# The seam before the last MLP by halves of the tokens, and where the last down weights are split

## The chip, the core and the metric

The kernel runs on one core of a Trainium2 chip. The time is device microseconds of one execution of the whole program; a lower one is better. A profiled execution gives the trace from which all rows below are taken. Five kinds of work appear in it: TensorE (PE, with its weight loads PEld apart), VectorE (DVE), ScalarE (ACT), GpSimd (POOL, hardly used here) and SyncE (SP), whose queue issues nearly all loads.

## What is computed

The reference is a two-layer backbone over 256 latent tokens and 256 context tokens, 1024 wide. Layer 0 mixes by a Conformer convolution, layer 1 by a bidirectional mLSTM with four heads. Each mixer and each MLP closes with a norm:

```python
h = layer_norm(ALPHA * h + g1 * y, ln1_g[i], ln1_b[i])
h = layer_norm(ALPHA * h + g2 * sq_relu_mlp(modulate(h, sh2, sc2), mlp_w1[i], mlp_w2[i]), ln2_g[i], ln2_b[i])

def sq_relu_mlp(u, w1, w2):
    return jnp.square(jax.nn.relu(u @ w1)) @ w2
```

The change lies at the end of layer 1, where only the 256 latent tokens are left: the mixer's last product (`y @ w_down`, one quarter of its input rows for each head), the norm over it, and the MLP (1024 to 4096 to 1024) with the last norm.

## The kernel before

Every f32 operand is split in two fp32r parts, a high one (ScalarE's cast, L154) and a low one (VectorE's subtraction, L155), and a product is taken as high x high, high x low and low x high. Weights come in raw tiles of 1 MB (`raw_load`, L148; three buffers, tag `raw`), each holding two pieces of 128x1024; `split_w` (L160) splits a piece into a `wh` and a `wl` tile (four buffers each, `NW`), or, if it is given a maker, into four tiles of 128x512 from that maker's pool. Nothing in the program fixes the order on an engine, but for a few marked places: a planner lays the instructions of each engine in a list ahead of time, by program order as priority and by its own estimates of when an operand is ready; the chip then runs each list in order. A tile made in a pool waits for the release of the tile that had its place.

The mixer's end is `down(h)` (L1371), once for each head: four k tiles, each with products for two token halves t (128 tokens) and two column halves h_ (512 columns), all into four PSUM banks `dacc`. Heads 0 to 2 run interleaved with the attention of head 3 (`Z.att`, last entry). Then four pieces of the MLP's first weights are loaded and split (`pre1`, L1431), and only then does `down(3)` load and split its weights, into the `XL` pool, whose sixteen tiles held the input of the output gate (`gate_o`, L1293) until the last gate was done. `down(3)` runs one (t, h_) after the other, and after each VectorE scales, adds and takes statistics (L1398 to L1400). `root` (L1410) makes mean and reciprocal deviation, L1445 normalizes in place, and L1448 transposes the tokens into four banks `trs` (two `ln`, two `cv`), each of which holds two of the eight feature tiles for both token halves. When both halves are in, `affine_half` (L492) makes each of the eight MLP inputs `u2[f]`: two ScalarE passes from PSUM over 256 tokens (L496) and a VectorE subtraction (L497); a `u2` tile holds the high part in columns 0 to 255 and the low part behind it.

The MLP's first four hidden tiles are made together: k tile outermost, four PSUM banks (three `mm`, one `fl`, the same that `dacc` had). `up_mm` (L1468) takes w high x both parts of u2 in one product of 512 columns (L1470) and w low x u2 high in one of 256 (L1471). `up_out` (L1479) adds the two halves, squares the positive part and splits it into `hid`. The loop then goes in steps of two hidden tiles m: `up(m)`, `up(m+1)`, `dn(m-4)`, `dn(m-3)`, where `dn` (L1513) adds a hidden tile's product with w2 to four banks `facc`. At m = 6 VectorE scales the residual by the rows `ln1g` and `ln1b` (L1537, L1538); these rows are loaded after the mixer's pool is closed. The last four `dn` run by (t, h_), each followed by the epilogue L1545 to L1547; after each token half come `root`, L1551, L1552 and the store.

Of the kernel before, what the change touches and what calls it, by code (L numbers as in the profile page):

```python
# [15 lines left out]
P = 128  # L16
# [7 lines left out]
H = 4  # L24
# [48 lines left out]
def hybrid_kernel(ctx: ExitStack, tc: tile.TileContext, xT, vecs_d, cc_d, rows_d, wdw_d, ada0_w, ada_w, ada1_w, wg_d, pw1a, pw1, pw2, w1_0, w2_0,  # L73
# [74 lines left out]
    def raw_load(src):  # L148
        raw = wp.tile([P, 2048], F32, tag="raw", name=nm("raw"), bufs=3)
        nc.sync.dma_start(raw[:, :src.shape[-1]], src)  # L150
        return raw
# [1219 lines left out]
    def down(h):  # L1371
        if h == 0:
            for t in range(2):
                for h_ in range(2):
                    dacc[t, h_] = psum("fl" if t and h_ else "mm")
            for h_ in range(2):
                g1r.append(PW())
                nc.sync.dma_start(g1r[h_], row(g_dr[0][h_ * T:(h_ + 1) * T]))
        last = h == H - 1
        ws = []  # L1380
        for q in range(2):
            raw = raw_load(wdown[h, q])
            for i in range(2):
                w = split_w(raw[:, i * D:(i + 1) * D], XL if last else None)
                ws.append(w if last else tuple([v_[:, h_ * T:(h_ + 1) * T] for h_ in range(2)] for v_ in w))
                if not last:
                    kt = 2 * q + i
                    for t in range(2):
                        for h_ in range(2):
                            down_mm(h, kt, t, h_, ws[kt])  # L1390
                    yield
        if last:
            for t in range(2):
                for h_ in range(2):
                    for kt in range(4):
                        down_mm(h, kt, t, h_, ws[kt])
# [4 lines left out]
                    yield  # L1401

    def down_mm(h, kt, t, h_, w):
        yh, yl = yy[h][kt]
# [31 lines left out]
    trs = []  # L1436
    last = down(H - 1)
    for t in range(2):
        for h_ in range(2):
            next(last)  # L1440
        root(mv1[:, t], st1[:, t])
        if t == 0:
            trs = [psum(n_) for n_ in ("ln", "ln", "cv", "cv")]
        for h_ in range(2):
            nc.vector.tensor_scalar(hl[t][h_], hl[t][h_], mv1[:, t, 0:1], mv1[:, t, 2:3], op0=ALU.subtract, op1=ALU.mult)  # L1445
            for j in range(4):
                f = 4 * h_ + j
                nc.tensor.transpose(trs[f // 2][:, f % 2 * C + t * P:f % 2 * C + (t + 1) * P],  # L1448
                                    hl[t][h_][:, j * P:(j + 1) * P], ident)
    for _ in last:  # L1450
        pass
    close_pool()

    ca, cb = comb(1, "ln1_g1", "ln1_b1", "sc2", "sh2", (1,))
    qf = open_pool("qf")
    U, HD = maker(qf, "u", DT), maker(qf, "hid", 8)
    u2 = []
    for f in range(DT):
        t = U(F32R)
        affine_half(t[:, LO], t[:, HI], trs[f // 2][:, f % 2 * C:f % 2 * C + C], 1, ca, cb, f)  # L1460
        u2.append(t)
# [32 lines left out]
    def weights2(j):  # L1494
        if j % 2 == 0:
            raws["d"] = raw_load(w2_1[j // 2])
        return split_w(raws["d"][:, j % 2 * D:(j % 2 + 1) * D])

    def up(m):
        w, ps = weights1(m), psum()  # L1500
# [15 lines left out]
            for h_ in range(2):  # L1516
                fin_mm(j, t, h_, w)

    pss = [psum("fl" if m == 3 else "mm") for m in range(4)]
    for kt in range(DT):  # L1520
        for m in range(4):
            up_mm(pss[m], pre1[m], kt)
    for m in range(4):
        up_out(m, pss[m])
    for t in range(2):
        for h_ in range(2):
            facc[t, h_] = psum("cv" if t else "ln")
    for m in range(4, NF, 2):
        up(m)
        up(m + 1)  # L1530
        dn(m - 4)
        dn(m - 3)
        if m == 6:
            for t in range(2):
                for h_ in range(2):
                    r, sl = hl[t][h_], slice(h_ * T, (h_ + 1) * T)
                    nc.vector.scalar_tensor_tensor(r, r, ALPHA, ln1g[:, sl], op0=ALU.mult, op1=ALU.mult)  # L1537
                    nc.vector.scalar_tensor_tensor(r, ln1b[:, sl], ALPHA, r, op0=ALU.mult, op1=ALU.add)  # L1538
    ws = [weights2(j) for j in range(NF - 4, NF)]
    for t in range(2):  # L1540
        for h_ in range(2):
            for j in range(NF - 4, NF):
                fin_mm(j, t, h_, ws[j - NF + 4])
            tm, r, sl = tmp("E"), hl[t][h_], slice(h_ * T, (h_ + 1) * T)
            nc.vector.tensor_tensor(tm, facc[t, h_], g2r[:, sl], op=ALU.mult)  # L1545
            nc.vector.tensor_tensor(r, r, tm, op=ALU.add)
            nc.vector.bn_stats(st1[:, t, h_, :], r)  # L1547
# [86 lines left out]
```

## Time and profile before

| | |
|---|---|
| median of three runs | 1727.58 us (1720.66, 1727.64, 1727.58) |
| the profiled execution | 1725.27 us, its span 1723.6 us |
| mean granted TensorE clock | 0.991 |
| PE busy | 1681.7 us (98%), 9450 products |
| DVE busy | 1052.4 us (61%) |
| ACT busy | 730.0 us (42%) |
| DMA | 301.64 MB, 175 GB/s in the mean |

A row of the timeline gives start and length in us, the engine, the line of the kernel, the operation with output and inputs, the shape, and in brackets how long the engine stood idle before it and what released it. A product's length covers its passage through the array, so lengths overlap, and the pace is read from the starts. A row of the windows gives busy time and number of instructions for each engine, then the granted TensorE clock, the share of time that the DMA engines were busy, and GB/s. A row of groups gives busy time, mean ns of one, and the idle time before.

### The profile page before, as it was taken

The numbers are of one execution on the slowest core, as the hardware profiler recorded it, in microseconds if no ns is written. First come the engines' busy times: TensorE is split into PE (matmuls) and PEld (weight loads), VectorE is DVE, ScalarE is ACT, GpSimd is POOL, SyncE is SP. The second block draws the span as 40 slices with busy tenths as digits, with TensorE's granted clock in tenths as the row PEclk, the third lists the DMA queues.
The fourth block names the chain that finished last, engine by engine and source line by source line (L and its number), as shares of the span: only waits on it lengthen the run. The fifth ranks groups of instructions, "written<-read, shape, count | busy, mean of one in ns | idle before, by whom it ended". The sixth has DMA issues, their size and how long they took to land.

```text
span 1723.6 us, 23808 instructions
## 1 busy us (share of the span) xinstructions
PE 1681.7 (98%) x9450; PEld 1400.1 (81%) x9450; DVE 1052.4 (61%) x1887; ACT 730.0 (42%) x1148; POOL 33.6 (2%) x84
## 2 busy tenths in 40 slices
PE   8999999999999999999999999999999999979997
PEld 5655798888888999986688999998777878868886
DVE  5456897975665776772132443443487776677666
ACT  3311763231324465542232432442476574445542
POOL 0000000000000000000000000000010110000000
PEclk9999999999999999999999999999999999989999
DMA  9323533665556055568653642343345555456552
GB/s 362 139 109 123 216 127 146 221 220 158 207 220 169 28 165 171 170 214 281 235 193 101 216 146 98 121 149 147 138 171 204 183 210 205 171 183 220 189 185 90
DMA packets 62687, 301.64 MB, mean 175 GB/s; under 512 B 8115, under 2 KB 22963, under 8 KB 29169
## 3 DMA queue, kind: packets, MB, share of 16 engines
q1 hardware_dynamic: 42832, 285.44, 47.0%
q10 hardware_dynamic: 19744, 14.69, 2.6%
q8 instruction: 74, 1.21, 0.3%
q14 instruction: 37, 0.30, 0.0%
HBM read 284.37 MB, written 15.74 MB: 174 GB/s over the span
## 4 chain that ended last, share of the span: by engine, by line
PE 91%; DVE 4%; ACT 2%; DMA 1%; issue 1%; POOL 0%; SPq 0%; DVEq 0%; ACTq 0%; POOLq 0%
PE mm L177 19%; PE mm L181 19%; PE mm L180 19%; PE mm L1470 3%; PE mm L185 3%; PE mm L187 3%; PE mm L186 3%; PE mm L1471 2%; PE cv L185 1%; PE cv L187 1%; PE cv L186 1%; PE fl L297 1%; DVE wl L155 1%; PE fl L647 1%; PE cv L716 1%; PE ln L177 1%
## 5 line engine op out<-in xcount | busy, mean ns | idle before, releaser
L155 DVE TENSOR_TENSOR wl<-raw,wh 128x1024 fp32r<-128x1024 f32 x350 | 427.0, 1223 | 357.0 <-ACT wh L154 354.4
L154 ACT CAST wh<-raw 128x1024 fp32r<-128x1024 f32 x350 | 364.9, 1050 | 560.6 <-PE mm L180 347.8
L180 PE MATMUL mm<-u,wh 128*128 128x256 f32 (+1 forms) x1152 | 376.9, 327 | 0.0
L177 PE MATMUL mm<-u,wh 128*128 128x256 f32 (+1 forms) x1024 | 328.2, 321 | 5.8 <-DVE E L673 2.9
L181 PE MATMUL mm<-u,wl 128*128 128x256 f32 (+1 forms) x1024 | 327.0, 320 | 0.0
L180 PEld LDWEIGHTS mm<-u,wh 128*128 128x128 f32 x1152 | 220.6, 192 | 18.1 <-DVE mv L482 0.8
L177 PEld LDWEIGHTS mm<-u,wh 128*128 128x128 f32 x1024 | 196.2, 192 | 27.6 <-issue 8.9
L181 PEld LDWEIGHTS mm<-u,wl 128*128 128x128 f32 x1024 | 196.4, 192 | 15.9 <-DVE wl L155 1.7
L177 PE MATMUL mm<-xm,wh 128*128 128x512 f32 x256 | 102.8, 402 | 0.0
L185 PE MATMUL mm<-wh,xl 128*128 128x512 f32 x256 | 101.3, 397 | 0.7 <-ACT wh L154 0.5
L186 PE MATMUL mm<-wh,xl 128*128 128x512 f32 x256 | 100.5, 392 | 0.6 <-DVE xl L155 0.6
L181 PE MATMUL mm<-xm,wl 128*128 128x512 f32 x256 | 100.3, 392 | 0.0
L187 PE MATMUL mm<-wl,xl 128*128 128x512 f32 x256 | 99.6, 394 | 0.3 <-DVE wl L155 0.2
L177 PE MATMUL mm<-hid,wh 128*128 128x512 f32 (+1 forms) x256 | 94.0, 367 | 2.2 <-ACT hid L154 2.2
L180 PE MATMUL mm<-hid,wh 128*128 128x512 f32 (+1 forms) x256 | 93.8, 367 | 0.1
L181 PE MATMUL mm<-hid,wl 128*128 128x512 f32 (+1 forms) x256 | 93.6, 366 | 0.0
L1470 PE MATMUL mm<-u,wh 128*128 128x512 f32 x248 | 89.2, 402 | 1.4 <-DVE u L497 1.0
L357 DVE CUSTOM_DVE_ANT_0 raw<-raw,cb,vecs 128x1024 f32<-128x1024 f32 x48 | 61.1, 1281 | 33.9 <-DMA raw<-ada_w 33.6
L180 PE MATMUL mm<-qq,wh 128*128 128x272 f32 x256 | 73.9, 289 | 0.0
L177 PE MATMUL mm<-qq,wh 128*128 128x272 f32 x256 | 73.9, 289 | 0.0
L181 PE MATMUL mm<-qq,wl 128*128 128x272 f32 x256 | 73.8, 288 | 0.0
L177 PEld LDWEIGHTS mm<-xm,wh 128*128 128x128 f32 x256 | 48.1, 188 | 22.5 <-issue 6.7
(462 smaller groups left out, 3064.2 us busy)
## 6 DMA issues: line engine op xcount, KB each, us to landing
raw<-w SPq DMA_DIRECT2D x64, 1024.0 KB, 4.8
raw<-ada_w SPq DMA_DIRECT2D x48, 1024.0 KB, 5.0
raw<-wo SPq DMA_DIRECT2D x32, 1024.0 KB, 4.8
raw<-wv SPq DMA_DIRECT2D x16, 1024.0 KB, 5.4
raw<-wqT SPq DMA_DIRECT2D x16, 1024.0 KB, 5.6
raw<-wq SPq DMA_DIRECT2D x16, 1024.0 KB, 4.8
raw<-wk SPq DMA_DIRECT2D x16, 1024.0 KB, 4.9
raw<-pw SPq DMA_DIRECT2D x10, 1024.0 KB, 7.0
```

The source lines that it names most:

```text
L154: c = nc.scalar.copy(hi, src)
L155: nc.vector.tensor_tensor(lo, src, hi.bitcast(F32), op=ALU.subtract)
L177: a = nc.tensor.matmul(ps, wh, xh, start=start, stop=False)
L180: nc.tensor.matmul(ps, wh, xl, start=False, stop=False)
L181: nc.tensor.matmul(ps, wl, xh, start=False, stop=stop)
L185: nc.tensor.matmul(ps, xh, wh, start=start, stop=False)
L186: nc.tensor.matmul(ps, xl, wh, start=False, stop=False)
L187: nc.tensor.matmul(ps, xh, wl, start=False, stop=stop)
L297: a = nc.tensor.matmul(ps[32 * j:32 * j + 32], cs[:, kt, 14 - 2 * v:46 - 2 * v], blocks[kt], start=first and kt < 4, stop=last and kt >= 4 ...
L357: nc.vector.tensor_tensor_reduce(dump, w, cb[:, s, :], 1.0, vecs[:, o:o + 1], ALU.mult, ALU.add, accum_out=ada[1][:, m, s:s + 1])
L1470: a = lambda stop: nc.tensor.matmul(ps, wh, u2[kt], start=kt == 0, stop=stop)
L1471: b = lambda: nc.tensor.matmul(ps[:, LO], wl, u2[kt][:, LO], start=False, stop=False)
```

## The change

1. `down(1)` loads the raw tiles of `down(3)`'s weights beside its own and splits them into the `XL` tiles, piece by piece behind its own products; `down(3)` then only multiplies.
2. `u2` lies in the pool of `x` tiles, which outlives the mixer's pools, and is made by token halves (`u2_half`), with 128 columns an operation. `turn(0)` and `u2_half(0)` stand ahead of the second token half's `down(3)` products in the program. The first four hidden tiles are made by `first(t, ...)`: for one token half, a product of 256 columns (128 tokens, high and low) and one of 128. The transposes `turn(1)` are issued behind the products of k tile 5 of the first half.
3. For the second token half the fourth hidden tile's products come after those of the other three.
4. The scaling of the residual moves from m = 6 to m = 8 and is tied there: its first instruction keeps its place in the program, and the others are issued behind it.
5. The pieces of w2 for j = 24 to 27 are loaded and split at m = 16 and 18 into sixteen tiles of their own (`wx`). `dn` is left out for j = 24 to 27; the last eight j run at the end: first token half with both column halves, then the second token half by column halves, each with its epilogue behind it.
6. `hid` has ten buffers instead of eight.

```diff
@@ down(h)
+        if h == H - 1:
             for t in range(2):
                 for h_ in range(2):
                     for kt in range(4):
-                        down_mm(h, kt, t, h_, ws[kt])
+                        down_mm(h, kt, t, h_, wlast[kt])
...
+        for q in range(2):
+            raw = raw_load(wdown[h, q])
+            if h == 1:
+                rawl = raw_load(wdown[H - 1, q])
+            for i in range(2):
...
+                        down_mm(h, 2 * q + i, t, h_, w)
+                if h == 1:
+                    wlast.append(split_w(rawl[:, i * D:(i + 1) * D], XL))
+                yield
@@ the seam
+    ca, cb = comb(1, "ln1_g1", "ln1_b1", "sc2", "sh2", (1,))
+    u2 = [X(F32R) for _ in range(DT)]
+
+    def u2_half(t):
+        for f in range(DT):
+            src = trs[f // 2][:, f % 2 * C + t * P:f % 2 * C + (t + 1) * P]
+            hi, lo, y = u2[f][:, t * P:(t + 1) * P], u2[f][:, C + t * P:C + (t + 1) * P], tmp("S")[:, :P]
+            for o_ in (hi, y):
+                nc.scalar.activation(o_, src, AF.Identity, scale=ca[:, 1, f:f + 1], bias=cb[:, 1, f:f + 1])
+            nc.vector.tensor_tensor(lo, y, hi.bitcast(F32), op=ALU.subtract)
+
+    def up_half(ps, w, kt, t):
+        wh, wl = kcol(w, kt)
+        v = lambda z_: z_.rearrange("p (s t) -> p s t", s=2)[:, :, t * P:(t + 1) * P]
+        a = lambda stop: nc.tensor.matmul(v(ps), wh, v(u2[kt]), start=kt == 0, stop=stop)
+        b = lambda: nc.tensor.matmul(ps[:, t * P:(t + 1) * P], wl, u2[kt][:, t * P:(t + 1) * P], start=False, stop=False)
+        if kt < DT - 1:
+            a(False)
+            return b()
+        b()
+        return a(True)
+
+    def first(t, grp, kts):
+        for kt in kts:
+            for m in grp:
+                a = up_half(pss[m], pre1[m], kt, t)
+        return a
+
+    def turn(t):
+        for h_ in range(2):
+            for j in range(4):
+                f = 4 * h_ + j
+                nc.tensor.transpose(trs[f // 2][:, f % 2 * C + t * P:f % 2 * C + (t + 1) * P],
+                                    hl[t][h_][:, j * P:(j + 1) * P], ident)
...
+        for h_ in range(2):
+            nc.vector.tensor_scalar(hl[t][h_], hl[t][h_], mv1[:, t, 0:1], mv1[:, t, 2:3], op0=ALU.subtract, op1=ALU.mult)
         if t == 0:
             trs = [psum(n_) for n_ in ("ln", "ln", "cv", "cv")]
+            turn(0)
+            u2_half(0)
     for _ in last:
         pass
+    pss += [psum("fl" if m == 3 else "mm") for m in range(4)]
+    mid = first(0, range(4), range(6))
+    with tc.issue_after(mid.ins):
+        turn(1)
+    first(0, range(4), range(6, DT))
+    u2_half(1)
+    first(1, range(3), range(DT))
+    first(1, (3,), range(DT))
     close_pool()
@@ the loop and the tail
     for m in range(4, NF, 2):
         up(m)
         up(m + 1)
-        dn(m - 4)
-        dn(m - 3)
+        if m < NF - 4:
+            dn(m - 4)
+            dn(m - 3)
+        if m == 8:
+            ops = scaled()
+            first = tc.keep_in_program_order(next(ops))
+            with tc.issue_after(first.ins):
+                for _ in ops:
+                    pass
+        if 16 <= m < 20:
+            for j in (NF - 24 + m, NF - 23 + m):
+                wend[j] = weights2(j, WX)
+    for j in range(NF - 4, NF):
+        w = weights2(j)
+        wend[j] = tuple([v_[:, h_ * T:(h_ + 1) * T] for h_ in range(2)] for v_ in w)
     for t in range(2):
+        for hs_ in ([(0, 1)] if t == 0 else [(0,), (1,)]):
+            for j in range(NF - 8, NF):
+                for h_ in hs_:
+                    yh = hid[j]
+                    mm3t(facc[t, h_], yh[:, t * P:(t + 1) * P], yh[:, C + t * P:C + (t + 1) * P], wend[j][0][h_], wend[j][1][h_],
+                         False, j == NF - 1)
```

`scaled` issues the same eight instructions as L1537 and L1538 before; `weights2(j, WX)` passes the maker to `split_w`.

More of the change, by code (lines that the diff above doesn't have):

```diff
@@ L1517, in dn @@
                 fin_mm(j, t, h_, w)
[L1519 to L1522, printed above, removed]
     for m in range(4):
@@ L1527, in hybrid_kernel, with scaled @@
             facc[t, h_] = psum("cv" if t else "ln")
+    def scaled():
+        for t in range(2):
+            for h_ in range(2):
+                r, sl = hl[t][h_], slice(h_ * T, (h_ + 1) * T)
+                yield nc.vector.scalar_tensor_tensor(r, r, ALPHA, ln1g[:, sl], op0=ALU.mult, op1=ALU.mult)
+                yield nc.vector.scalar_tensor_tensor(r, ln1b[:, sl], ALPHA, r, op0=ALU.mult, op1=ALU.add)
+    wend = {}
     for m in range(4, NF, 2):
```

49 lines of the change are left out of this document (10 added, 39 removed).

## The prediction, made before the changed kernel was run

> **What bounds the kernel now.** I read the windows first: for most of the span TensorE has no gap, and what can be won lies where it has one.
>
> ```profile
> core 0: us, PE busy (x) PEld busy (x) DVE busy (x) ACT busy (x) POOL busy (x), PEclk, DMA share, GB/s
> 1508.80:1512.80 4.00, 0.23 (x2) 0.02 (x1) 2.98 (x4) 2.10 (x4) 0.00 (x0) 1.00 0.88 373
> 1512.80:1526.80 14.00, 13.98 (x56) 10.46 (x56) 12.15 (x21) 3.97 (x8) 0.00 (x0) 0.88 0.69 259
> 1603.00:1614.08 11.08, 11.08 (x58) 9.41 (x57) 7.27 (x10) 5.55 (x8) 0.00 (x0) 1.00 0.55 192
> ```
>
> The row at 1603 is one step of the MLP loop (two `up`, two `dn`): TensorE full, VectorE 7.27 of 11.08 us. The rows above it are the seam, where TensorE stands still and then runs at a granted clock of 0.88. Next the timeline of TensorE through the seam:
>
> ```profile
> 1508.62 0.39 PE L187 MATMUL fl<-wl,x 128*128 128x512 f32 x1
> 1512.78 0.78 PE L185 MATMUL mm<-xl,og 128*128 128x512 f32 x1 [3.77 <-ACT xl L154]
> 1513.36 0.63 PE L186 MATMUL mm<-xl,og 128*128 128x512 f32 x1
> ...
> 1519.90 0.39 PE L187 MATMUL mm<-xl,og 128*128 128x512 f32 x1
> ...
> 1525.07 0.63 PE L1448 MATMUL ln<-ident,hl 128*128 128x128 f32 x4
> 1525.54 0.60 PE L1448 MATMUL cv<-ident,hl 128*128 128x128 f32 x4
> ...
> 1526.43 0.40 PE L187 MATMUL fl<-xl,og 128*128 128x512 f32 x1
> 1530.42 1.12 PE L1448 MATMUL ln<-ident,hl 128*128 128x128 f32 x4 [3.59 <-DVE hl L1445]
> 1533.41 0.79 PE L1470 MATMUL mm<-u,wh 128*128 128x512 f32 x1 [1.02 <-DVE u L497]
> ...
> 1537.80 0.39 PE L1470 MATMUL mm<-u,wh 128*128 128x512 f32 x1
> 1538.03 0.28 PE L1471 MATMUL mm<-u,wl 128*128 128x256 f32 x1
> 1538.15 0.39 PE L1470 MATMUL mm<-u,wh 128*128 128x512 f32 x1
> ...
> 1545.90 0.39 PE L1470 MATMUL fl<-u,wh 128*128 128x512 f32 x1
> 1546.66 0.50 PE L1470 MATMUL mm<-u,wh 128*128 128x512 f32 x1 [0.37 <-ACT wh L154]
> 1547.92 0.39 PE L1471 MATMUL mm<-u,wl 128*128 128x256 f32 x1 [0.76 <-DVE wl L155]
> ```
>
> Starts are closer than durations, since products overlap: 0.23 us for 512 columns (1537.80 to 1538.03), 0.12 for 256 (1538.03 to 1538.15), so 0.35 for a pair L1470 and L1471. After the 3.77 us gap a product of 512 columns lasts 0.63 us where it lasts 0.39 later, so 0.24 is lost with each: half speed. From 1508.85 (the last product of the third `down` done) to 1546.13 (the last first product) 37.3 us pass, for 48 x 0.227 + 16 x 0.105 + 32 x 0.35 = 23.8 us of work. The 13.5 us between are three waits and the slow clock after them.
>
> **The change, part by part.** I lay the new order on the time axis of this trace. The sum is made against the profiled execution, 1725.27 us (span 1723.6 and 1.67 around it); the median of the runs shown, 1727.58, is 2.3 above it, and those runs spread over 7 us (1720.66 to 1727.64).
>
> *Last w_down split early.* The first wait follows from the load order:
>
> ```profile
> L155 DVE TENSOR_TENSOR wl<-raw,wh 128x1024 fp32r<-128x1024 f32 x350 | 427.0, 1223 | 357.0 <-ACT wh L154 354.4
> L154 ACT CAST wh<-raw 128x1024 fp32r<-128x1024 f32 x350 | 364.9, 1050 | 560.6 <-PE mm L180 347.8
> ...
> 1491.83 0.33 SPq L150 DMA_DIRECT2D raw<-wdown  x1
> 1507.24 0.89 SPq L150 DMA_DIRECT2D raw<-wdown  x2
> raw<-wdown SPq DMA_DIRECT2D x8, 1024.0 KB, 4.8
> ACT wh L154 <- PE fl L186: 16.7, 6, 4.4
> ```
>
> With two loads of 4.8 us moved ahead of the third `down` and of `pre1` on SP's queue, the 3.77 us and the half speed behind it go. What is late next is the last head's own output, whose low half VectorE ends at 1510.6 (the next fence); two of four k tiles are ready by then, which last 6 x 0.227 = 1.4 us, to 1510.2. I put 0.5 us there. The 8 casts and 8 subtractions of 512 columns (at most 0.7 each, as L155 in the next fence) move into a stage where ScalarE waits 16.7 us in six waits for TensorE: nothing. But three raw buffers now carry two more loads before those of the third `down`. Its first load takes the buffer of a moved one; that one lands about 1484.5 and needs four casts and subtractions, so I estimate 1489.5, landing at 1494.3, split (1.05 and 1.22, the two rows on top) by 1496.7. The first use, counted back from 1508.85 by 48 x 0.227 and eight transposes, is 1497.1. If it gets the buffer freed at 1491.83 instead, it is 1.9 us late, and twice that if the other is late too. Bounds 0 and 3.8 us lost; I take 0.7, as the near case just fits.
>
> *Half norms.*
>
> ```profile
> 1509.92 0.68 DVE L155 TENSOR_TENSOR og<-og,og 128x512 fp32r<-128x512 f32 x1
> 1531.72 1.29 DVE L1537 SCALAR_TENSOR_TENSOR hl<-hl,row 128x512 f32<-128x512 f32 x2 [0.90 <-DMA row<-rows_d]
> 1531.69 0.56 ACT L496 ACTIVATE S<-ln,cb,ca 128x256 f32<-128x256 f32 x1
> 1532.14 0.56 ACT L496 ACTIVATE u<-ln,cb,ca 128x256 fp32r<-128x256 f32 x1
> 1497.62 1.52 ACT L1347 ACTIVATE og<-og,gmv 128x512 f32<-128x512 f32 x2
> L1257 DVE TENSOR_TENSOR S<-S,x 128x128 f32<-128x128 f32 x8 | 2.3, 281 | 0.0
> ```
>
> Tokens 0 to 127 end at 1508.85 + 0.5 + 24 x 0.227 = 1514.8. Today their norm takes 5.0 us (1520.1 to the transposes at 1525.07), so `turn(0)` stands at 1519.6, among the products of the other tokens, which end at 1521.1. ScalarE: 256 columns pass every 0.45 us, 512 every 0.72 (1.52 less 0.8, its mean), so about 0.32 for 128 (estimate), 0.64 for one of the eight u2 tiles, and 0.28 for its subtraction on VectorE. The first tile is there at about 1521.2: TensorE goes on with almost no gap. The two L1537 that the planner had put ahead of the u2 subtractions, waiting for a row's load, are now tied to step m = 8, where VectorE has 3.8 of 11.08 us free and the eight instructions take 5.4; the weights run three tiles ahead, so I charge 0.2 us (0 to 1.5).
>
> *The price of the half products.* 32 pairs of 512 and 256 columns become 64 pairs of 256 and 128, each with its own weight load. No row has a 128-column product of this type. Below, the weight load alone sets the pace; above stands the plain f32 product, which runs as two instructions:
>
> ```profile
> 1258.14 0.41 PE L1187 MATMUL ln<-E,ones 128*128 128x128 f32 x2
> 1258.39 0.29 PE L1186 MATMUL ln<-E,tri 128*128 128x16 f32 x2
> 1258.53 0.37 PE L1187 MATMUL ln<-E,ones 128*128 128x16 f32 x2
> 1258.75 0.48 PE L187 MATMUL mm<-wl,xl 128*128 128x512 f32 x1
> 199.00 0.59 PE L413 MATMUL ln<-ln,inv_h 128*128 128x256 f32 x2
> 199.43 0.50 PE L441 MATMUL ln<-inv_c,ln 128*128 128x1 f32 x4
> ```
>
> Even 16 columns cost 0.11 us each (1258.53 to 1258.75 for two), the transposes of 128 columns 0.12 (1525.07 to 1525.54 for four). Plain f32 costs 0.25 at 128 columns (1258.14 to 1258.39) and 0.43 at 256. By share of columns alone it would be 0.06. I take 0.11, since the transposes are nearest in shape and single instructions: a pair is 0.23, and 64 pairs 14.7 us against 11.2, 3.5 us of new TensorE work. Bounds of the pair: 0.17 and 0.37 (0.12 + 0.25).
>
> The Trainium skill, "TensorE: Matmul & The Clock Gate", section "Back-to-back issue gap", gives about 81 ns for each of a stream of weight loads with 128 columns; the 0.11 of the rows above is dearer. By it a pair were 0.20, the first products ended 1.9 us sooner than below, and the time came to about 1713.1; an estimate from that page. The rows decide, since their weights are 4 bytes wide too.
>
> *The sum of the seam.* Six k tiles of `first(0)`: 24 x 0.23 = 5.5, to 1526.7. The other norm takes 3.6 us from the last product (1526.83 to 1530.42), plus up to 1.8 behind half-tile subtractions: ready at 1524.7 to 1526.5, so `turn(1)` at 1526.7 doesn't wait; this cover of up to 2 us is lost if the products are cheaper. It ends at 1527.6, the two last k tiles at 1529.4. ScalarE makes a tile each 0.64 us from 1527.2, done at 1532.3; TensorE needs 32 x 0.23 = 7.4 and sets the end: 1536.8 against 1546.13, 9.3 us gained. Behind it, today's gaps (0.53 and 1.03 us) come from a copy, cast and subtraction (some 0.4, 1.05 and 1.22) that start when all four tiles end. The fourth tile's products now come last and cover 8 x 0.23 = 1.84 us: about 0.6 stays, 1.0 gained.
>
> *The tail.*
>
> ```profile
> 1713.60 0.39 PE L187 MATMUL cv<-wl,hid 128*128 128x512 f32 x1
> 1713.73 1.28 DVE L1545 TENSOR_TENSOR E<-cv,row 128x512 f32<-128x512 f32 x2
> 1719.08 1.41 DVE L1552 SCALAR_TENSOR_TENSOR E<-hl,mv,row 128x512 f32<-128x512 f32 x2
> ```
>
> VectorE ends 6.5 us after the last product (1713.99 to 1720.49), behind three doubled operations. Now 24 products (5.4 us) of the last half cover all of the third quarter; left are three operations of 0.65 (1.28 for two), four of 0.7 (1.41 for two) and some 0.6 of statistics and handing over, 5.4: 1.1 us gained (0.5 to 1.5). The w2 splits into `WX` at m = 16 and 18 add a third load per step: 192 GB/s becomes about 285, and 373 is seen above; a load has 8 us from buffer to use against 4.8. Nothing, or up to 1 us.
>
> Sum: 9.3 + 1.0 + 1.1 - 0.7 - 0.2 = 10.5; 1725.27 - 10.5 = 1714.8 us.
>
> **The rivals.**
>
> *Short products at the plain f32 price.* A pair is 0.35 to 0.37. By 0.35, `first(0)`'s six tiles end at 1529.6, `turn(1)` at 1530.5, the rest after 40 x 0.35 = 14.0 at 1544.5: 1.6 gained, then 1.5 and 1.1, less 0.9: 3.3, so 1722.0. For it: no product of this type under 256 columns is in the trace. Against it: 16 to 128 columns cost 0.11 to 0.12 per instruction, whatever their number.
>
> *Short products by their columns.* Pair 0.17: the u2 tiles of ScalarE then set the pace, the end is at 1533.4, and the time about 1711.8. Against it stands the 16-column row.
>
> *The order on TensorE.* The planner places `turn(0)` ahead of the other tokens' products. TensorE then stands from 1514.8 to 1519.6 and restarts at half speed (1.6 us, as after the 3.77): the first products end at 1543.2, and the time is 1721. For it: the planner moved L1537 ahead of what was needed. Against it: in this trace it left `turn(0)`'s predecessor, 1525.07, behind 45 of 48 products.
>
> *Late weights in the third `down`.* 1.9 to 3.8 us lost instead of 0.7: 1716 to 1718.
>
> *Slower.* The 256-column products with their two strided parts of 128 also fall to the plain price: 0.43 + 0.25 = 0.68 a pair, 64 x 0.68 + 0.9 = 44.4, an end at 1565.6, 19.5 later, less 1.7 won elsewhere: 1743. It turns to a loss from 0.40 a pair. Against it: L1186 writes 128 columns in four parts at the same price.
>
> **How the numbers follow.** Forecast (1712.5 to 1717) 0.52; plain f32 price 0.16; order 0.07; late weights 0.09; cheap products 0.09; slower 0.07. About 0.5% (8.6 us against 1727.58, so 1718.9) is what can be told from no change. Faster: forecast, cheap products and most of late weights, 0.68. Same: plain price, order and the rest, 0.25. Slower 0.07. The range runs from the cheap products with a low run, 1709, to the plain price with a little above, 1723.
>
> **What would show it.** Right: no gap over 1 us on TensorE between the third `down` and the MLP loop, a granted clock of 1.00 throughout, 128-column products 0.11 us apart, first products ended about 28 us after the third `down`, and 5.4 us of VectorE after the last product. Wrong: starts of 0.2 us or more behind 128-column products; a wait of `turn(0)` or `turn(1)` for the norm; waits of the third `down` for `wh` or `wl`; new waits at m = 8, 16 or 18.

## The result, and the profile after

| | before | after |
|---|---|---|
| median | 1727.58 us (1720.66 to 1729.26, 5 runs) | 1713.61 us (1711.55 to 1715.58, 5 runs) |
| span of the profiled execution | 1723.55 us | 1709.67 us |

The ratio is 0.9926, 95% interval 0.9904 to 0.9948: faster by 0.74%, 9.0 to 16.6 us by the interval. The forecast was 1714.8 us.

The two profiled executions differ by 13.9 us, and not all of that belongs to the change. The window near 557 us, in code that the change doesn't touch, in the kernel before:

```profile
core 0: us, PE busy (x) PEld busy (x) DVE busy (x) ACT busy (x) POOL busy (x), PEclk, DMA share, GB/s
557.00:560.60 3.60, 3.60 (x20) 3.60 (x20) 1.39 (x3) 0.00 (x0) 0.00 (x0) 0.53 0.90 360
```

TensorE ran 3.6 us at a granted clock of 0.53 there, with 20 products of 256 columns; after, the same window has a clock of 1.00 and 32 products. That is 1.7 us. In all the third `down` ends 2.1 us earlier (1506.77 against 1508.85). Nothing in the traces puts any of it down to the change: in the window near 557 us the kernel after with the old tail, further below, has a clock of 0.53 again. In the 208.85 us before the third `down` ends, where the early loads and splits now lie, TensorE is busy for 208.62 us, where it was 208.66, so they cost it nothing there. Over the executions below this moment lies anywhere from 1506.28 to 1512.96. So I read each part from the end of the third `down` on, and 11.8 us are the change's.

TensorE through the seam of the kernel after, in its timeline:

```profile
1506.54 0.39 PE L187 MATMUL fl<-wl,x 128*128 128x512 f32 x1
1506.77 0.39 PE L185 MATMUL mm<-xl,og 128*128 128x512 f32 x1
...
1516.51 0.63 PE L1473 MATMUL ln<-ident,hl 128*128 128x128 f32 x4
...
1518.57 0.39 PE L187 MATMUL fl<-xl,og 128*128 128x512 f32 x1
1518.80 0.28 PE L1453 MATMUL mm<-x,wh 128*128 128x256 f32 x1
1518.92 0.22 PE L1454 MATMUL mm<-x,wl 128*128 128x128 f32 x1
1518.98 0.33 PE L1453 MATMUL mm<-x,wh 128*128 128x256 f32 x1
1519.15 0.22 PE L1454 MATMUL mm<-x,wl 128*128 128x128 f32 x1
1519.21 0.34 PE L1453 MATMUL mm<-x,wh 128*128 128x256 f32 x1
...
1524.65 0.61 PE L1473 MATMUL ln<-ident,hl 128*128 128x128 f32 x4
...
1534.62 0.33 PE L1453 MATMUL fl<-x,wh 128*128 128x256 f32 x1
1534.79 0.39 PE L1509 MATMUL mm<-x,wh 128*128 128x512 f32 x1
1535.31 0.38 PE L1510 MATMUL mm<-x,wl 128*128 128x256 f32 x1
```

No row carries a releaser in brackets: the last `down` (L185 to L187) follows the third (1506.54 to 1506.77) without a gap, the first products (L1453, L1454) follow the last `down` (1518.57 to 1518.80), and `turn(0)` and `turn(1)` (the two rows L1473) stand among products. The first products end at 1534.79, where the fifth tile's first product starts. That is 28.02 us after 1506.77; before it was 37.27. Of the wait that follows, 0.29 us is left (1535.31 less 1534.79 less 0.23 for 512 columns). The windows of the same stretch, of a later step of the loop and of the tail:

```profile
core 0: us, PE busy (x) PEld busy (x) DVE busy (x) ACT busy (x) POOL busy (x), PEclk, DMA share, GB/s
1506.77:1518.80 12.03, 11.97 (x57) 9.76 (x56) 9.30 (x17) 3.18 (x8) 0.00 (x0) 1.00 0.58 231
1518.80:1534.80 16.00, 15.85 (x138) 15.70 (x136) 8.53 (x24) 11.85 (x35) 0.00 (x0) 1.00 0.49 165
1598.50:1609.58 11.08, 11.08 (x58) 9.41 (x57) 9.68 (x15) 7.27 (x12) 0.00 (x0) 1.00 0.67 243
1701.30:1709.70 8.40, 0.04 (x1) 0.00 (x0) 5.09 (x9) 0.29 (x1) 0.00 (x0) 0.68 0.17 62
```

The last `down` takes 12.03 us where it took 13.88, at a clock of 1.00 instead of 0.88. In the 16 us of first products TensorE is busy for 15.85, and the weight load for nearly all of it, 15.70. The loop step at 1598.50, one of those with added w2 splits, still takes 11.08 us with TensorE full. The tail, from the last product to the end of the span, is 8.33 us where it was 9.57.

| from | before | after | gain | forecast |
|---|---|---|---|---|
| end of third `down` to end of first products | 37.27 | 28.02 | 9.25 | 9.3 |
| waits before the fifth tile's products | 1.56 | 0.29 | 1.27 | 1.0 |
| rest of the loop, to the last product | 166.30 | 166.26 | 0.04 | -0.2 |
| last product to the end of the span | 9.57 | 8.33 | 1.24 | 1.1 |
| late weights in the third `down` | | | 0 | -0.7 |
| sum | | | 11.8 | 10.5 |

### The profile page after: what moved, and what is told of

The parts are those of the page before. It is cut to its first block, busy times and chain, and to the rows that moved or that the text cites. A ratio compares the mean times of both kernels' runs of the same rounds, so it can differ in the third digit from the quotient of the medians.

```text
span 1709.7 us, 23961 instructions
## 1 busy us (share of the span) xinstructions
PE 1678.7 (98%) x9514; PEld 1401.4 (82%) x9514; DVE 1051.9 (62%) x1899; ACT 734.1 (43%) x1168; POOL 33.6 (2%) x84
## 4 chain that ended last, share of the span: by engine, by line
PE 87%; DVE 5%; DMA 4%; ACT 2%; issue 1%; POOL 0%; SPq 0%; DVEq 0%; ACTq 0%; POOLq 0%
PE mm L177 17%; PE mm L181 17%; PE mm L180 17%; DMA raw<-ada_w 3%; PE mm L187 3%; PE mm L185 3%; PE mm L1509 3%; PE mm L186 3%; PE cv L186 2%; PE cv L185 2%; PE cv L187 2%; PE mm L1510 2%; DVE wl L155 1%; PE fl L297 1%; PE fl L647 1%
## 5 line engine op out<-in xcount | busy, mean ns | idle before, releaser
L155 DVE TENSOR_TENSOR wl<-raw,wh 128x1024 fp32r<-128x1024 f32 x346 | 421.9, 1223 | 346.6 <-ACT wh L154 344.2
L154 ACT CAST wh<-raw 128x1024 fp32r<-128x1024 f32 x346 | 360.7, 1050 | 546.3 <-PE mm L180 350.1
L185 PE MATMUL mm<-wh,xl 128*128 128x512 f32 x256 | 101.3, 397 | 0.7 <-ACT wh L154 0.5
L187 PE MATMUL mm<-wl,xl 128*128 128x512 f32 x256 | 99.7, 395 | 0.3 <-DVE wl L155 0.2
L1509 PE MATMUL mm<-x,wh 128*128 128x512 f32 x224 | 79.0, 397 | 0.0
```

The source lines that it names most:

```text
L154: c = nc.scalar.copy(hi, src)
L155: nc.vector.tensor_tensor(lo, src, hi.bitcast(F32), op=ALU.subtract)
L185: nc.tensor.matmul(ps, xh, wh, start=start, stop=False)
L187: nc.tensor.matmul(ps, xh, wl, start=False, stop=stop)
L1509: a = lambda stop: nc.tensor.matmul(ps, wh, u2[kt], start=kt == 0, stop=stop)
```

## The experiments

A part of the change is worth a few us, and executions of one kernel differ by as much. So the parts are read from the traces, from the end of the third `down` on, and "seam" below is the first row of the table. By the timed runs alone, the kernels that were run five times or more are faster than the kernel before, but none of them stands clear of the kernel after: the intervals of their ratios all overlap with its 0.9904 to 0.9948.

### One part alone: the early split

The kernel before, with the last w_down loaded and split during the second `down`, and nothing else.

```diff
+            if h == 1:
+                rawl = raw_load(wdown[H - 1, q])
...
+                if h == 1:
+                    wlast.append(split_w(rawl[:, i * D:(i + 1) * D], XL))
```

> The kernel before with one part of the change: the weights of the last head's down product are loaded and split beside those of head 1. Theory (the terms of the sum add): the wait of 3.77 us before the last down product and the half speed behind it (8 products, 0.24 us each, 1.9 us) go, the wait for the norm (3.6 us) and what follows stay. From the end of the third down product to the end of the first MLP products 37.3 us become about 31.6; the time falls by 5.5 us. Rival (the early split is the whole gain): it falls by 10 us or more, since what follows starts earlier too. Rival (the wait comes back at another place): by less than 2 us.

Measured: 1718.72 us (1717.64 to 1723.24, 6 runs) against 1725.67 for the kernel before on that chip (13 runs): ratio 0.9963 (0.9948 to 0.9977). Seam 32.25 us. TensorE in the timeline of this kernel:

```profile
1527.40 0.66 PE L1451 MATMUL ln<-ident,hl 128*128 128x128 f32 x4 [3.59 <-DVE hl L1448]
...
1530.28 0.80 PE L1473 MATMUL mm<-u,wh 128*128 128x512 f32 x1 [1.77 <-DVE u L497]
```

The last `down` starts without a gap and takes 12.03 us, and the seam loses 5.0 us. The time fell by 4.0 to 9.0 us by the interval of the ratio, so neither rival (10 us and more, or 2 and less) is near. The wait for the norm (3.59 us) and that for the first u2 tile stay, the second longer than before (1.77 against 1.02), and half speed behind them too: the first product lasts 0.80 us.

### Everything but the early split

The kernel after, with the last w_down loaded and split at the head of `down(3)`, as before.

```diff
         if h == H - 1:
+            for q in range(2):
+                raw = raw_load(wdown[h, q])
+                for i in range(2):
+                    wlast.append(split_w(raw[:, i * D:(i + 1) * D], XL))
...
-            if h == 1:
-                rawl = raw_load(wdown[H - 1, q])
...
-                if h == 1:
-                    wlast.append(split_w(rawl[:, i * D:(i + 1) * D], XL))
```

> The changed kernel with the last weights loaded and split late again, as before; all else stays. Theory: the wait of about 3.8 us and the half speed behind it (1.9 us) are back, the seam goes from 28.0 to 33.5 us, the time is 5.5 us above the changed kernel's. Rival (the early split is the whole gain): 10 us above. Rival (the halves cover this wait too): less than 2 us above.

Measured: 1718.44 us (1716.43 to 1724.14, 7 runs), ratio 0.9959 (0.9945 to 0.9974). Seam 34.86 us, 6.8 more than after. A row of the timeline, and one of the windows (with the columns shown above):

```profile
1511.50 0.80 PE L185 MATMUL mm<-xl,og 128*128 128x512 f32 x1 [3.67 <-ACT xl L154]
```

```profile
1511.50:1526.50 15.00, 14.98 (x56) 11.61 (x56) 12.44 (x22) 5.09 (x12) 0.00 (x0) 0.79 0.62 244
```

The wait of 3.67 us for ScalarE's cast is back, and the half speed behind it lasts 6.8 us here, not the 3.4 us of the kernel before. The clock of 0.79 over 15 us costs 3.1 us, and with the wait this is the 6.8. The expectation was right in kind and a little low, because it took the half speed to be as short as before.

### Without the halves by tokens

The kernel after, with the first products over all 256 tokens, behind both norms.

```diff
         if t == 0:
             trs = [psum(n_) for n_ in ("ln", "ln", "cv", "cv")]
-            turn(0)
-            u2_half(0)
+        turn(t)
...
-    mid = first(0, range(4), range(6))
-    with tc.issue_after(mid.ins):
-        turn(1)
-    first(0, range(4), range(6, DT))
-    u2_half(1)
-    first(1, range(3), range(DT))
-    first(1, (3,), range(DT))
+    for f in range(DT):
+        affine_half(u2[f][:, LO], u2[f][:, HI], trs[f // 2][:, f % 2 * C:f % 2 * C + C], 1, ca, cb, f)
+    for grp in (range(3), (3,)):
+        for kt in range(DT):
+            for m in grp:
...
+                    a(False)
+                    b()
```

> The changed kernel with whole tokens in the seam: both norms first, then u2 over 256 tokens and products of 512 and 256 columns (32 pairs instead of 64); the early split, the fourth tile last, the rows at m = 8 and the new tail stay. Theory: TensorE saves 3.5 us of short products but waits 3.6 us for the second norm and 1.3 us for the first u2 tile, and runs part of the first products at half speed: the seam goes from 28.0 to between 29.0 and 30.6 us, the time is 1 to 2.6 us above the changed kernel's. Rival (the short products eat what the halves hide): the same or faster than the changed kernel, seam 28 us or less.

Measured: 1717.11 us (1713.07 to 1721.58, 7 runs), ratio 0.9949 (0.9928 to 0.9969). Seam 31.56 us. Timeline and windows:

```profile
1522.07 0.66 PE L1473 MATMUL ln<-ident,hl 128*128 128x128 f32 x4 [3.59 <-DVE hl L1482]
...
1524.08 0.80 PE L1495 MATMUL mm<-x,wh 128*128 128x512 f32 x1 [0.67 <-DVE x L497]
```

```profile
1524.10:1537.90 13.80, 13.80 (x65) 12.01 (x66) 5.82 (x13) 9.18 (x20) 0.00 (x0) 0.80 0.26 101
```

The halves are worth 3.5 us in the seam (31.56 less 28.02), 3.2 us with the wait of 0.29 us behind it, which this kernel doesn't have, though they add TensorE work: 32 pairs of full width would take 11.2 us at full speed, 64 short ones take 14.8. The full ones took 13.8, at a clock of 0.80, after two waits of 4.3 us in all. The seam lies above the range that was expected, for the same reason as in the run before: the half speed lasted 6.8 us again. Between the early split alone and this kernel (32.25 and 31.56) lie the new places of the scalings and of `comb`, and the fourth tile's products behind the others: 0.7 us together, and the wait for the first u2 tile is 0.67 instead of 1.77.

### Is it the gap that makes the half speed?

The kernel before, with 18 products into a bank that isn't used, where TensorE waits for the last w_down. They stand for work that would fill the gap; their result is not used.

```diff
+    fill = psum("cv")
+    for i in range(18):
+        nc.tensor.matmul(fill, pre1[0][0][:, 0:P], pre1[1][0][:, 0:T], start=True, stop=True)
     last = down(H - 1)
```

> The kernel before with 18 products of 512 columns into an unused PSUM bank (4.1 us at 0.227 each) ahead of the last down product, so that TensorE is busy while it waits for the weights; their result is not used. Theory (the gap itself makes the half speed): the weights come at the same time, the first down products then run 0.23 us apart instead of 0.42, and the seam falls from 37.3 to 35.4 us. Rival (the half speed belongs to the first products on fresh tiles, not to the gap): the starts stay 0.42 us apart, and the seam does not fall.

Measured: 1722.83 us (one run), seam 35.89 us. Timeline:

```profile
1507.40 4.24 PE L1439 MATMUL cv<-wh,wh 128*128 128x512 f32 x18
1511.48 0.39 PE L185 MATMUL mm<-xl,og 128*128 128x512 f32 x1
...
1523.53 0.63 PE L1451 MATMUL ln<-ident,hl 128*128 128x128 f32 x4 [1.01 <-DVE hl L1448]
```

The last `down` starts as late as before (4.08 us after the third ended) but now at full speed: its first product lasts 0.39 us instead of 0.78, and the whole 10.88 us instead of 13.88. So the gap itself makes the half speed, and filling it, even with nothing useful, takes it away. Of these 3.0 us the half speed is 1.85: at full speed, with the eight transposes of the first token half among its products as before, the `down` takes 12.03 us (the early split alone). The other 1.15 us is that these transposes now stand behind the `down` (the row at 1523.53), where they wait for VectorE. The seam wins 1.4 us. What became of the 1.15, VectorE's timeline shows at the last tile's first operation, in the kernel before and then in this one:

```profile
1526.87 0.69 DVE L1398 TENSOR_TENSOR E<-fl,pw 128x512 f32<-128x512 f32 x1 [0.89 <-PE fl L187]
```

```profile
1523.75 0.68 DVE L1398 TENSOR_TENSOR E<-fl,pw 128x512 f32<-128x512 f32 x1
```

Before, VectorE waits for the product and starts 0.2 us after the `down` ends (1526.66). Here the `down` ends at 1522.36, and VectorE, which has no idle time ahead of the row, comes to it 1.4 us later. The faster `down` has made VectorE's norms the next to be late, and the other norm follows the `down` 1.2 us later than before.

### What sets the price of a short product

The kernel after, with the 128-column product widened to the 256 columns (high and low halves) of the other; it computes one small term more.

```diff
-        b = lambda: nc.tensor.matmul(ps[:, t * P:(t + 1) * P], wl, u2[kt][:, t * P:(t + 1) * P], start=False, stop=False)
+        b = lambda: nc.tensor.matmul(v(ps), wl, v(u2[kt]), start=False, stop=False)
```

> The changed kernel with the 128-column products of the seam (w low x u2 high) doubled to 256 columns (w low x u2 high and low; one small term more is computed than the reference needs). Theory (a short product costs its weight load): a pair of products stays at 0.23 to 0.24 us, the seam at 28.0 to 28.7. Rival (a short product costs its columns): 128 columns more in 64 products, 0.053 us each, 3.4 us: a pair of 0.28, the seam at 31.4 us.

Measured: 1717.65 us (one run). Timeline:

```profile
1523.43 0.28 PE L1453 MATMUL mm<-x,wh 128*128 128x256 f32 x1
1523.55 0.28 PE L1454 MATMUL mm<-x,wl 128*128 128x256 f32 x1
1523.67 0.28 PE L1453 MATMUL mm<-x,wh 128*128 128x256 f32 x1
...
1539.01 0.49 PE L1509 MATMUL mm<-x,wh 128*128 128x512 f32 x1 [0.88 <-ACT wh L154]
1540.10 0.38 PE L1510 MATMUL mm<-x,wl 128*128 128x256 f32 x1 [0.59 <-DVE wl L155]
```

A pair now takes 0.24 us (1523.43 to 1523.67) where it took 0.23 after (1518.98 to 1519.21), and the seam is 28.34 instead of 28.02. Twice the columns in half of the products cost 0.3 us over 64 pairs; by columns the seam would have been 31.4. So below 256 columns the price no longer follows the columns. It is about 0.115 us, and the rows point to the weight load, of which every product has its own: loads are busy for 15.70 of 16.00 us in the window of the kernel after, and there they start evenly (1519.03, 1519.15, 1519.26), where the products don't. In the kernel before, a load of 32 columns lasts 108 ns, one of 64 columns 135 and one of 128 columns 188, which is 0.83 ns a column, or 0.107 us for 128. No run takes the loads away, so this part is read and not tested.

Behind the seam this run lost 3.1 us more (169.66 us to the last product, after it was 166.55), and that was not expected: the planner put other work ahead of the next tiles' splits on ScalarE and VectorE (waits of 0.88 and 0.59 us), and 3.4 us of half speed came after them. That is taken up again below.

### The fourth tile's products last

The kernel after, with the second halves of all four tiles together.

```diff
-    first(1, range(3), range(DT))
-    first(1, (3,), range(DT))
+    first(1, range(4), range(DT))
```

> The changed kernel with the second token half's first products over four hidden tiles at once, not the fourth tile last. Theory: all four tiles' weights come free at the end, so copy, cast and subtraction (0.4, 1.05 and 1.22 us) stand bare again: waits of about 0.5 and 1.0 us ahead of the fifth tile's products instead of 0.3, 1.2 us in all. Rival (the weights of the fifth tile are late for another reason): the same wait of 0.3 us.

> The same kernel as with four tiles together before, run anew because that execution ran with TensorE at half speed nearly throughout. Theory: about 0.5 and 1.0 us of waits ahead of the fifth tile's products, 1.2 us more than in the changed kernel in all; seam 28.0 us. Rival: the same wait of 0.3 us as in the changed kernel.

The first of the two executions ran at a mean granted clock of 0.557 and took 2774 us; why is open, and nothing is read from it. The second, the same kernel: 1717.58 us (one run), seam 28.02 us as after. Timeline and windows:

```profile
1538.36 0.50 PE L1508 MATMUL mm<-x,wh 128*128 128x512 f32 x1 [0.72 <-ACT wh L154]
1539.62 0.39 PE L1509 MATMUL mm<-x,wl 128*128 128x256 f32 x1 [0.76 <-DVE wl L155]
```

```profile
core 0: us, PE busy (x) PEld busy (x) DVE busy (x) ACT busy (x) POOL busy (x), PEclk, DMA share, GB/s
1537.00:1540.40 3.40, 1.93 (x11) 1.35 (x10) 2.91 (x6) 3.40 (x8) 0.00 (x0) 1.00 0.00 0
1540.40:1544.00 3.60, 3.60 (x13) 3.10 (x12) 3.31 (x8) 2.49 (x4) 0.00 (x0) 0.53 0.13 20
```

The waits are back, 1.6 us more than after by the starts of the products (1.2 were expected), and 3.4 us of half speed with them, which the theory hadn't: 169.72 us from the end of the first products to the last product instead of 166.55. Holding the fourth tile back is worth 1.3 us against the waits of the kernel before, and 3.2 us in this one execution of the new order, where the waits cost the clock as well.

### The scalings without their tie

The kernel after, with the eight scalings issued at step 6 and not tied to their place.

```diff
-        if m == 8:
-            ops = scaled()
-            first = tc.keep_in_program_order(next(ops))
-            with tc.issue_after(first.ins):
-                for _ in ops:
-                    pass
+        if m == 6:
+            for _ in scaled():
+                pass
```

> The changed kernel with the eight scalings of the residual at m = 6 and without a fixed place, as before. Theory: the planner puts them on VectorE among the second half's subtractions, where they wait for their rows' loads and then take 0.65 us each; TensorE waits 0.5 to 1.5 us at the first products of the second token half, and the loop gives nothing back. Rival (they cost nothing there, since TensorE is behind VectorE by then): the seam stays at 28.0 us.

Measured: 1718.34 us (one run), seam 28.43, the loop 166.55 us as after. VectorE's timeline:

```profile
1530.20 1.29 DVE L1567 SCALAR_TENSOR_TENSOR hl<-hl,row 128x512 f32<-128x512 f32 x2
```

The planner put them into the seam again, among the u2 subtractions, but they cost only 0.4 us there, just under the least that was expected: VectorE has the room. The tie to step 8 is worth little in this order of work. The execution as a whole is longer than that of the kernel after because its third `down` ended at 1512.96, before any of this.

### The old tail

The kernel after, with the last four w2 blocks and the order of the last tiles as before.

```diff
-        if m < NF - 4:
-            dn(m - 4)
-            dn(m - 3)
+        dn(m - 4)
+        dn(m - 3)
...
-        for hs_ in ([(0, 1)] if t == 0 else [(0,), (1,)]):
-            for j in range(NF - 8, NF):
-                for h_ in hs_:
...
         for h_ in range(2):
+            for j in range(NF - 4, NF):
+                yh = hid[j]
```

> The changed kernel with the tail as before: four hidden tiles at the end, by token half and column half, no w2 pieces split at m = 16 and 18. Theory: from the last product to the end of the span it takes 9.6 us again instead of 8.4, and the loop ahead is as long as in the changed kernel (166.0 us from the fifth tile to the last product). Rival (the early w2 splits cost the loop what the tail wins): the loop is shorter by 0.5 us or more.

Measured: 1715.52 us (one run). Tail 9.59 us, as before (9.57), and the stretch from the first products' end to the last product 166.59 as after (166.55). The new tail gains 1.25 us in the tail and costs nothing in the loop, where four pieces of w2 are loaded and split ahead of their use.

### The fourth tile whole

The experiments point to one thing to gain still: the fourth tile comes last, behind both norms, so its products need not be halved.

```diff
-    mid = first(0, range(4), range(6))
+    mid = first(0, range(3), range(7))
     with tc.issue_after(mid.ins):
         turn(1)
-    first(0, range(4), range(6, DT))
+    first(0, range(3), (7,))
     u2_half(1)
     first(1, range(3), range(DT))
-    first(1, (3,), range(DT))
+    for kt in range(DT):
+        wh, wl = kcol(pre1[3], kt)
...
+            a(False)
+            b()
```

> The changed kernel with the fourth hidden tile in whole tokens at the end (8 pairs of 512 and 256 columns for 16 of 256 and 128); the other three by halves, the transposes of the second half behind k tile 6. Theory (each half pair costs 0.23 us and a whole one 0.35): 16 x 0.231 less 8 x 0.347, 0.9 us saved, a wait of about 0.2 us at the transposes new, and the 0.3 us ahead of the fifth tile gone: from the third down product's end to the fifth tile's second product 27.3 to 27.6 us instead of 28.5; the time equal to the changed kernel's within what can be measured. Rival (the fewer covering products leave TensorE waiting for the second half's u2): 28.5 us or more.

Measured: 1711.91 us (1709.98 to 1715.48, 5 runs) against 1726.38 (9 runs) for the kernel before on that chip: ratio 0.9917 (0.9903 to 0.9930). Seam 27.10 us; to the fifth tile's second product, as the expectation counts it, 27.34 us.

Eight full pairs (0.35 us) take the place of 16 short ones (0.23): 0.9 us, as expected, and with the loop 1.3 us by the trace. The ratio's interval contains that of the kernel after, so in the timed runs this isn't shown to be better than it.

### Together

| part | us | from |
|---|---|---|
| early split | 5.0 | seam 37.27 to 32.25, alone |
| new places of scalings and `comb`, order of products | 0.7 | 32.25 to 31.56 |
| halves by tokens | 3.5 | 31.56 to 28.02 |
| fourth tile last | 1.3 | waits 1.56 to 0.29 |
| last tiles by tokens | 1.25 | tail 9.59 to 8.33 |

The sum is 11.75, and the traces of before and after differ by 11.8 in the same stretches. The parts depend on their order: the early split taken away last costs 6.8 instead of 5.0.

## Why the prediction was right

*The last w_down early.* Right: the gap and the half speed went. The wait of 0.5 us for the last head's own output was not there, and neither were the 0.7 us for late weights in the third `down`. The rows of the kernel after, on VectorE, on SP's queue, on ScalarE and of the waits:

```profile
1505.22 0.68 DVE L155 TENSOR_TENSOR og<-og,og 128x512 fp32r<-128x512 f32 x1
```

```profile
1485.52 0.33 SPq L150 DMA_DIRECT2D raw<-wdown  x1
1489.76 0.33 SPq L150 DMA_DIRECT2D raw<-wdown  x1
```

```profile
1490.37 2.00 ACT L154 CAST wh<-raw 128x1024 fp32r<-128x1024 f32 x2 [1.89 <-DMA raw<-wdown]
```

The low half of the last head's output ends at 1505.9, 0.9 us before its use, where the prediction had laid it 1.7 us behind the third `down`'s end: in the planner's order before, VectorE came to it only behind a weight split that itself waited for ScalarE's cast, and that order is another one now. The loads of the third `down` were issued at 1485.5 and 1489.8. On the time axis of before the first is 1487.6, about 1.9 us ahead of the estimated 1489.5, and ScalarE, which waited 1.89 us for it, casts both blocks by 1492.4; TensorE has no wait for them. The buffer came free earlier than was laid out, and the far case, with the rival that rested on it, fell.

*Half norms.* Right. `turn(0)` went out at 1516.51 among the other tokens' products, the first u2 tile was there when those ended, and `turn(1)` didn't wait:

```profile
1523.08 1.00 DVE L1482 TENSOR_SCALAR hl<-hl,mv 128x512 f32<-128x512 f32 x2
```

The other norm is ready at 1524.08, 17.3 us after the third `down`, inside the 15.9 to 17.7 that were laid out, and `turn(1)` starts at 1524.65. That is a cover of 0.6 us, less than the "up to 2". ScalarE's price for 128 columns was estimated at 0.32 us:

```profile
1518.00 0.46 ACT L1447 ACTIVATE S<-ln,cb,ca 128x128 f32<-128x128 f32 x1
1518.34 0.47 ACT L1447 ACTIVATE x<-ln,cb,ca 128x128 fp32r<-128x128 f32 x1
```

The starts are 0.34 apart, near enough, and TensorE set the pace.

*The price of the half products.* Right as a pair, 0.23, and wrong in one detail of what was to show it: the 128-column products are not 0.11 us apart from what follows. The product of 256 columns starts 0.06 us after the short one (1519.15 to 1519.21), and the next short one 0.17 us after that (1518.98 to 1519.15). Two weight loads fit into 0.23 us whichever way the products share them, and the widened short products (0.12 and 0.12) settle that it isn't the columns. The Trainium skill, "TensorE: Matmul & The Clock Gate", section "LDWEIGHTS (loading the stationary operand)", puts a weight load at its columns over 1.2 in ns, by which 128 columns are estimated at 107 ns; the 0.115 us here agree with it within a tenth. The 81 ns of the section "Back-to-back issue gap", weighed in the prediction, were not reached: by its pair of 0.20 the 64 pairs would take 12.8 us, and they took 14.8. The measurement decides. The rival by columns falls with it, as does the plain f32 price in both its forms; and with `turn(0)` in its place so does the order on TensorE.

*Seam and waits behind it.* The seam, forecast at 28.0 us, was 28.02. Two small errors cancel in it: the last `down` was to take 12.25 us with its wait of 0.5 and took 12.03 without one, and the first products with `turn(1)` were to take 15.7 and took 15.99. Of the wait that follows, 0.29 us stay instead of 0.6.

*Scalings and loop.* The 0.2 us for the scalings at step 8 and the up to 1 us for third loads per step were not lost: 166.26 us without the waits, against 166.30, and the step with the added splits had TensorE full at 243 GB/s, where 285 was estimated.

*The tail.* Forecast: 5.4 us of VectorE after the last product, gain 1.1.

```profile
1700.95 0.39 PE L187 MATMUL cv<-wl,hid 128*128 128x512 f32 x1
1701.37 0.69 DVE L1598 TENSOR_TENSOR E<-cv,row 128x512 f32<-128x512 f32 x1 [2.65 <-PE cv L187]
...
1705.19 1.41 DVE L1605 SCALAR_TENSOR_TENSOR E<-hl,mv,row 128x512 f32<-128x512 f32 x2
```

From 1701.34 to 1706.60 it is 5.3 us, and 1.24 us were gained. That VectorE waited 2.65 us for the last product shows that all of the third quarter was done by then.

*The clock.* A granted clock of 1.00 throughout held in the kernel after, from the third `down` to the end of the loop. Where my own expectations of the experiments failed, it was here: I took the half speed behind a gap to last 3.4 us, as after the first gap of before, and it lasted 6.8 us in four of the kernels (early split alone, everything but it, whole tokens, gap filled), as it had behind the second gap of before. The prediction also took 0.24 us as lost with each product at half speed, from the lengths; by the starts (0.43 against 0.23) it is 0.20. The forecast did not depend on either, since it had no gap.

The median, 1713.61, lies 1.2 us under the forecast, and by the traces the change gained 1.3 us more than the sum: 0.7 for the late weights, which weren't late, 0.3 of the wait, 0.2 in the loop and 0.1 in the tail. All are mis-sized terms of a right sum. That the time itself was met so closely is in part luck: the sum was taken from the profiled execution, 2.3 us under the median before, and 10.5 us less than that median would have been 1717.1. The medians themselves differ by 14.0 us, more than the 11.8 of the traces; the interval of the ratio, 9.0 to 16.6, holds both.

## What to carry to other kernels

A short wait of TensorE costs more than itself where half speed follows; it pays to fill or remove it even at the price of more TensorE work, as the halved first products did here (3.6 us of added work, and still 3.5 us won in the seam). A product with a weight load of its own, of 128 columns, cost at least about 0.11 us here, however few its other columns, so halve only those products that have to be ready early, and leave whole what comes last anyway. When a stage is reordered, look again at the waits just behind it: waits of 1.6 us cost just that in the kernel before, while a little more of them, with the same products, cost 1.5 us of clock besides.

## What was not expected of the hardware

*Half speed without a long gap.* Before, TensorE waited for 0.37 and 0.76 us ahead of the fifth tile's products and kept its full clock. With the four tiles together (0.72 and 0.76) and with the widened short products (0.88 and 0.59), two waits that are hardly longer were followed by some 3.4 us at half of it. In every trace here the changes of the granted clock lie whole multiples of 3.41 us apart; in the kernel before, half speed runs from 557.11 to 560.52, from 1512.84 to 1516.25 and from 1529.90 to 1536.73. So I count TensorE's work in the 3.41 us that end at such a step. With the four tiles together and with the widened products it was 1.94 us, and half speed followed. With the early split alone, where both waits of the kernel before (0.37 and 0.76 us) lie in one such stretch, it was 2.27, and none followed. A bound between the two would fit the seam, but it does not hold elsewhere. Near 557 us, in the kernel without the halves and then in that without the tie of the scalings, each row with the one after it:

```profile
core 0: us, PE busy (x) PEld busy (x) DVE busy (x) ACT busy (x) POOL busy (x), PEclk, DMA share, GB/s
553.44:556.85 3.41, 1.68 (x14) 1.69 (x15) 2.13 (x4) 0.62 (x1) 0.00 (x0) 1.00 0.88 315
556.85:560.26 3.41, 3.41 (x31) 3.41 (x30) 0.98 (x3) 0.00 (x0) 0.00 (x0) 1.00 0.77 296
```

```profile
554.70:558.11 3.41, 1.83 (x11) 1.43 (x11) 3.41 (x6) 2.53 (x5) 0.00 (x0) 1.00 0.18 46
558.11:561.52 3.41, 2.21 (x10) 2.22 (x11) 1.28 (x3) 0.62 (x1) 0.00 (x0) 0.50 0.89 351
```

After 1.68 us of work the clock stayed at 1.00, and after 1.83 in the same code it fell to 0.50. So TensorE's busy time in the rows alone does not decide it, and what does is open. The Trainium skill, "TensorE: Matmul & The Clock Gate", section "Part 1: The HAM clock gate (the "warmup" mystery)", has a gate that goes by how busy TensorE was in a window of about 3.4 us, and the clock halved after an idle one. The lengths of the slow stretches here, 3.4 and 6.8 us, agree with a window of this size. That the window has to be idle doesn't: TensorE was busy for 57% of the 3.4 us ahead of one of them.

*How long half speed lasts.* Behind the first gap of the kernel before, TensorE was busy for the whole of the first 3.41 us at half speed, and the clock rose at their end. Behind its second gap and in four of the experiments, TensorE was busy for only 1.77 to 2.77 us of them, and half speed went on for another 3.41 us. By these six cases the price of a gap's half speed, 1.7 or 3.4 us, hangs on where TensorE starts again between two steps, which differs from one execution to the next (the first gap of before cost 3.4 us at half speed there, and its like 6.8 us in the kernel with everything but the early split). No run was made to test it, and half speed went on near 61 us in the early split alone, though TensorE was busy throughout.
